# Semaphores allocated and cleared by the kernel itself, in two steps on GpSimd, instead of by the surrounding tile context

## The chip, the cores and the metric

One core of one Trainium2 chip. The metric is device microseconds of one execution. The profiled execution is one run of its own; the other times are of runs without a profile.

## The reference

What is computed is a low-rank update that is added to its input, for 16 x 512 = 8192 tokens of width 768, with rank 16:

```python
def reference(x, A, B, scale):
    lora = np.matmul(np.matmul(x, A), B)
    return (x + scale * lora).astype(np.float32)
```

x and the output are float32 and 25.2 MB each; A and B are 48 KB each.

## The kernel before, in words

The tokens are cut into five parts of 8, 8, 16, 16 and 16 tiles of 128 tokens (`PARTS`, L14). SyncE issues every transfer (`on_sync`, L126): seven loads of x, one of A, one of B, and six stores. The buffer `x_all` holds 48 of the 64 tiles, so the last part's two loads wait until the first two stores have landed (`s_out0`, `s_out1`, L154 to L157). Work goes in eight groups of eight tiles. For each group ScalarE and GpSimd narrow x to float16 (`narrowed`, L163, instruction at L171), VectorE transposes the group (L229), TensorE multiplies by A (`projected`, L260) and by B (`raised`, L281), ScalarE moves the small product between the two with the scale (L217), and VectorE adds the result to x in place (`summed`, L234). TensorE runs the first seven groups in a loop (L302). The order on each engine is written out by hand, and engines wait for one another on semaphores with names that begin with `s_`.

The end of the kernel matters here. `s_sum` counts the groups at whose end a store may go; its sixth count comes with the last sum. SyncE waits for it before each store (L133) and issues the last store (L137), which counts in `s_out` like the three before it. All of the body stands in a critical section of the tile context, opened at L124 and closed at L320. Ahead of the close GpSimd waits until `s_out` is 64, that is, until the last four stores have landed (L319). The wait is carried by GpSimd's jump out of the section, which the profile puts at L124. Behind the jump GpSimd and SyncE pass a no-operation to each other (L124). Then the tile context closes (L351): a barrier of all engines, a clear of a range of semaphores by GpSimd, and a second barrier. The semaphores come from `tc.alloc_semaphore` (L77 and L78), so they belong to the tile context, and its clear covers them: numbers 99 to 129 are the kernel's 31, and 130 to 135 are six of the context's own, for the start and the end of the section.

Of the kernel before, what the change touches and what calls it, by code (L numbers as in the profile page):

```python
# [24 lines left out]
def kernel(  # L25
# [8 lines left out]
    nc = tc.nc  # L34
# [19 lines left out]
    def ps(name, shape):  # L54
        return nc.alloc_psum_tensor(name, shape, fp32).ap()
# [18 lines left out]
    lora = [ps(f"lora_ps{i}", [P, 2, D]) for i in range(2)]  # L74
    y_ps = ps("ps_yt", [P, GROUP, Q])

    def sem(name):  # L77
        return tc.alloc_semaphore(name)  # L78


    parts = []
# [14 lines left out]
    def tiles(t, n):  # L96
# [3 lines left out]
        (0, 0, 2), (0, 2, 6), (1, 0, 8), (2, 0, 16), (3, 0, 16), (4, 0, 8), (4, 8, 8)  # L100
    ]
    s_load = [sem(f"s_load{k}") for k in range(len(LOADS))]

    def load_of(t):
        i, s = where[t]
        return next(k for k, ld in enumerate(LOADS) if ld[0] == i and ld[1] <= s < ld[1] + ld[2])

    s_a, s_b = sem("s_a"), sem("s_b")
    s_ready, s_brows, s_pick = sem("s_ready"), sem("s_brows"), sem("s_pick")
    s_w, s_bh, s_bp, s_bm = sem("s_w"), sem("s_bh"), sem("s_bp"), sem("s_bm")  # L110
    s_first, s_narrow, s_turned, s_taken = sem("s_first"), sem("s_narrow"), sem("s_turned"), sem("s_taken")
    s_y, s_spread, s_lora = sem("s_y"), sem("s_spread"), sem("s_lora")

    s_free = [sem(f"s_free{p}") for p in range(PAIRS)]
    s_sum = sem("s_sum")
    s_out0, s_out1, s_out = sem("s_out0"), sem("s_out1"), sem("s_out")

    MMS = 2 * NC
    STORES = [(0, 0, 8), (1, 0, 8), (2, 0, 16), (3, 0, 16), (4, 0, 8), (4, 8, 8)]
# [1 line left out]
    STORED = [where.index((i, s + n - 1)) // GROUP for i, s, n in STORES]  # L121
# [194 lines left out]
    on_vector(nc.vector)  # L316
    on_tensor(nc.tensor)

    nc.gpsimd.wait_ge(s_out, (len(STORES) - 2) * 16)  # L319
    section.close()  # L320


# [33 lines left out]
```

## Time and profile before

| | us |
|---|---|
| median of 3 runs | 124.40 |
| lowest and highest of them | 124.37, 124.55 |
| the profiled execution, its time | 124.31 |
| its span, first to last instruction | 122.5 |
| around its span | 1.8 |
| VectorE busy, share of the span | 81.8 (67%) |
| TensorE busy | 50.7 (41%) |
| ScalarE busy | 38.9 (32%) |
| GpSimd busy | 27.3 (22%) |

How to read it: the span runs from the first to the last instruction of the program on any engine, and what lies around it belongs to the runtime. Busy time counts an engine's work on data alone. Branches, semaphore instructions, clears and the issuing of transfers belong to an engine's queue (its sequencer). They are marked with a "q" behind the engine's name (POOLq is GpSimd's, SPq SyncE's, PEldq TensorE's) and are not counted as busy. In the answers for one line of the code, the columns are the shortest, the median and the longest duration in ns, and then the first and the last start in us. Where a start is given to three places, it is the record's own, in us from the span's start; the trace also holds an event for each write to a semaphore, with its number and time.

### The profile page before, as it was taken

Reading aid. Unit: us, or ns where it says so; the run is one execution under the profiler, and the core shown is the slowest. Engines: PE = TensorE matmul, PEld = TensorE weight load, DVE = VectorE, ACT = ScalarE, POOL = GpSimd, SP = SyncE. Lnnn points to the kernel's source line nnn. Section 1 sums busy time; section 2 is a strip of 40 time slices with the busy share of each in tenths; the row PEclk is TensorE's granted clock in tenths of the full one; section 3 lists DMA queues with packets and bytes.
Section 4 is the critical chain, followed back from the end, with each engine's and each line's share of the span. In section 5 each row is a group of like instructions: output and inputs, shape, how many; then the busy total and the mean of one; then the engine's idle time right before and its main releaser. Section 6 shows DMA issues by size and latency. Waiting matters only on the chain.

```text
span 122.5 us, 883 instructions
## 1 busy us (share of the span) xinstructions
PE 50.7 (41%) x322; PEld 29.9 (24%) x322; DVE 81.8 (67%) x42; ACT 38.9 (32%) x44; POOL 27.3 (22%) x25
## 2 busy tenths in 40 slices
PE   0000219477104974574574576477467432000000
PEld 0000017244002642442332334244244211000000
DVE  0000960799509999999999999999999599100000
ACT  4131946700094454444264083172300400000000
POOL 7500666200080440440260080071000000000000
PEclk9999999999965799999999999999999999855555
DMA  3999997996997997999999999999799799799990
GB/s 60 419 439 389 425 562 305 514 498 273 514 498 321 465 498 305 457 401 433 465 385 441 457 409 465 417 498 465 321 498 482 337 482 465 321 465 401 425 465 24
DMA packets 1928, 50.43 MB, mean 412 GB/s; under 512 B 236, under 2 KB 236, under 8 KB 392
## 3 DMA queue, kind: packets, MB, share of 16 engines
q1 hardware_dynamic: 1928, 50.43, 96.6%
HBM read 25.26 MB, written 25.17 MB: 412 GB/s over the span
## 4 chain that ended last, share of the span: by engine, by line
DVE 49%; DMA 24%; issue 4%; POOL 3%; PE 2%; SPq 2%; POOLq 0%; DVEq 0%
DVE x_sb L234 33%; DMA x_sb<-in_x_dram 24%; DVE xt L229 16%; POOL xn L171 2%; PE lora_ps L281 1%; PE ps_yt L260 1%; POOL a_rows L176 1%; SPq L142 1%; SPq L129 0%; SPq L146 0%; POOLq L351 0%; DVEq L247 0%; SPq L124 0%
## 5 line engine op out<-in xcount | busy, mean ns | idle before, releaser
L234 DVE TENSOR_TENSOR x_sb<-x_sb,lora_ps 128x1536 f32<-128x1536 f32 x32 | 53.7, 1735 | 1.4 <-PE lora_ps L281 1.4
L281 PE MATMUL lora_ps<-b_mm,y_bd 128*128 128x512 f16 (+1 forms) x128 | 26.1, 339 | 26.5 <-issue 18.8
L171 ACT CAST xn<-x_sb 128x3072 f16<-128x3072 f32 (+1 forms) x10 | 24.9, 2495 | 37.9 <-DMA x_sb<-in_x_dram 20.9
L229 DVE STREAM_TRANSPOSE xt<-xn 128x3072 f32<-128x3072 f32 (+1 forms) x9 | 27.1, 3007 | 9.3 <-POOL xn L171 9.0
L260 PE MATMUL ps_yt<-xt,w_bd 128*128 128x256 f16 x192 | 25.3, 282 | 11.5 <-DVE xt L229 11.5
L171 POOL CAST xn<-x_sb 128x3072 f16<-128x3072 f32 x7 | 19.2, 2748 | 46.4 <-PE ps_yt L260 32.8
L260 PEld LDWEIGHTS ps_yt<-xt,w_bd 128*128 128x128 f16 x192 | 18.7, 100 | 18.9 <-issue 14.6
L281 PEld LDWEIGHTS lora_ps<-b_mm,y_bd 128*128 128x128 f16 x128 | 11.0, 100 | 39.5 <-issue 21.6
L217 ACT ACTIVATE y_bd<-ps_yt 32x256 f16<-32x256 f32 x32 | 12.0, 374 | 19.0 <-PE ps_yt L260 18.7
L222 DVE STREAM_TRANSPOSE a_t<-a_rows 96x1024 f32<-96x1024 f32 x1 | 2.0, 1964 | 12.0 <-DMA a_rows<-in_A_dram 12.0
L293 PE MATMUL lora_ps<-b_half,pick 128*128 128x512 f16 (+1 forms) x2 | 0.8, 500 | 13.3 <-POOL b_half L188 13.3
L293 PEld LDWEIGHTS lora_ps<-b_half,pick 128*128 128x128 f16 x2 | 0.1, 106 | 13.3 <-issue 13.3
L188 POOL CAST b_half<-b_rows 128x768 f16<-128x768 f32 x1 | 0.8, 824 | 7.5 <-DMA b_rows<-in_B_dram 7.5
L198 POOL COPY w_bd<-w_one 32x384 f16<-32x384 f16 x4 | 2.0, 501 | 0.2
L171 ACT ACT_TABLE_LOAD x1 | 1.3, 1283 | 0.9 <-SPq L124 0.9
L192 POOL CAST w_one<-a_t 32x128 f16<-32x128 f32 x3 | 1.2, 397 | 1.0 <-DVE a_t L222 0.9
L179 POOL MEMSET w_bd<- 128x1536 f32 x1 | 1.4, 1382 | 0.0
L176 POOL MEMSET a_rows<- 96x1024 f32 x1 | 0.9, 948 | 0.5 <-SPq L124 0.5
L210 ACT CAST b_mm<-lora_ps 128x768 f16<-128x768 f32 x1 | 0.8, 798 | 0.0
L177 POOL MEMSET b_rows<- 128x768 f32 x1 | 0.7, 736 | 0.0
L180 POOL MEMSET y_bd<- 128x512 f32 x1 | 0.5, 524 | 0.0
L182 POOL TENSOR_SCALAR_AFFINE_SELECT pick<-pick 128x128 f16<-128x128 f16 x1 | 0.3, 309 | 0.0
(5 smaller groups left out, 0.6 us busy)
## 6 DMA issues: line engine op xcount, KB each, us to landing
x_sb<-in_x_dram SPq DMA_DIRECT2D x2, 6144.0 KB, 36.8
out_dram<-x_sb SPq DMA_DIRECT2D x4, 3072.0 KB, 17.2
out_dram<-x_sb SPq DMA_DIRECT2D x2, 6144.0 KB, 22.9
x_sb<-in_x_dram SPq DMA_DIRECT2D x3, 3072.0 KB, 14.7
x_sb<-in_x_dram SPq DMA_DIRECT2D x1, 2304.0 KB, 10.4
x_sb<-in_x_dram SPq DMA_DIRECT2D x1, 768.0 KB, 4.7
a_rows<-in_A_dram SPq DMA_DIRECT2D x1, 48.0 KB
b_rows<-in_B_dram SPq DMA_DIRECT2D x1, 48.0 KB, 9.4
```

What stands on the lines that cost most here:

```text
L142: e.dma_start(out=a_rows[0 : NC * APART : APART, :], in_=A.rearrange("(c e) r -> c (e r)", e=64)).then_inc(s_a, 16)
L171: ins = copy(out=xn[:, ds(first, n), :], in_=tiles(t, n))
L176: e.memset(a_rows[0 : NC * APART], 0.0).then_inc(s_ready, 1)
L179: e.memset(w_bd.rearrange("p c k m -> p (c k m)").bitcast(fp32), 0.0)
L192: e.tensor_copy(out=w_one[:, ds(b * EACH, EACH), :, :], in_=a_t[ds(b * Q, Q)].rearrange("i k r (c n) -> i c k r n", n=APART)[..., 0],).the ...
L198: e.tensor_copy(out=w_bd[ds(b * Q, Q), :, :, ds(b * Q, R)], in_=w_one).then_inc(s_w, 1)
L217: last = e.mul(out=y_bd[q, :, q], in_=y_ps[q, :, :], mul=sc)
L222: e.transpose(out=a_t[0 : NC * APART].rearrange("i k r c -> i (k r) c"), in_=a_rows[0 : NC * APART].rearrange("c (i k r) -> c (k r) i", k= ...
L229: return e.transpose(out=ts[0], in_=ts[1])
L234: ins = e.tensor_tensor(out=xs, in0=xs, in1=lora[p % 2], op=mybir.AluOpType.add)
L260: mm = e.matmul(y_ps, w_bd[:, c, k, :], xv[:, :, c, :, k], start=(m == 0), stop=(m == MMS - 1),)
L281: mms.append(e.matmul(t[:, k, ds(n0, w)], y_bd[:, 2 * p + k, :], b_mm[:, ds(n0, w)], start=True, stop=True,))
```

## The change

The semaphores are taken from the core's allocator (`nc.alloc_semaphore`) and not from the tile context, which therefore no longer clears them. `s_sum` is moved behind `s_out0` and `s_out1`, so that the 29 others have the numbers 99 to 127, and `s_sum` and `s_out` have 128 and 129. At the end GpSimd waits until `s_sum` is 6 (the last sum is made) and clears 99 to 127. Then it waits until `s_out` is 64 and clears 128 and 129. The section's close and the context's close follow as before; the context's clear is left with 130 to 135.

```diff
+    sems = []
+
     def sem(name):
-        return tc.alloc_semaphore(name)
+        sems.append(nc.alloc_semaphore(name))
+        return sems[-1]
...
-    s_sum = sem("s_sum")
-    s_out0, s_out1, s_out = sem("s_out0"), sem("s_out1"), sem("s_out")
+    s_out0, s_out1 = sem("s_out0"), sem("s_out1")
+
+    s_sum, s_out = sem("s_sum"), sem("s_out")
...
+    nums = [s.num for s in sems]
+    assert nums == list(range(nums[0], nums[0] + len(nums))) and sems[-2:] == [s_sum, s_out]
+
+    nc.gpsimd.wait_ge(s_sum, len(STORED))
+    nc.gpsimd.sem_clear(range(nums[0], s_sum.num))
     nc.gpsimd.wait_ge(s_out, (len(STORES) - 2) * 16)
+    nc.gpsimd.sem_clear(range(s_sum.num, s_out.num + 1))
     section.close()
```

In the program that is built, GpSimd's first clear carries the wait for `s_sum` and the second the wait for `s_out`. The jump out of the section, which carried the wait for `s_out` before, waits for nothing now. The other engines' instructions are the same in number and order.

## The prediction

> **What bounds the kernel now.** I read the row of the DMA engines first, then the chain of waits at its end, then the last microseconds instruction by instruction. The span's 40 slices (3.06 us each) show the transfers busy from the second slice to the last but one; the only queue is at 96.6% of the 16 engines' span:
>
> ```profile
> span 122.5 us, 883 instructions
> ...
> DMA  3999997996997997999999999999799799799990
> ...
> q1 hardware_dynamic: 1928, 50.43, 96.6%
> ```
>
> The chain, followed in time, ends with VectorE's last four sums:
>
> ```profile
> 97.76 6.75 DVE x_sb L234 x4
> ```
>
> That is 97.76 + 6.75 = 104.51 us, 18 us ahead of the end. All that comes behind it is the last stores (the last one issued at 104.5) and a tail. The stretches of the last three microseconds show where data stop:
>
> ```profile
> 119.80:120.20 0.40, 0.00 (x0) 0.00 (x0) 0.00 (x0) 0.00 (x0) 0.00 (x0) 0.50 0.30 123
> 120.20:120.60 0.40, 0.00 (x0) 0.00 (x0) 0.00 (x0) 0.00 (x0) 0.00 (x0) 0.50 0.00 0
> 120.60:121.00 0.40, 0.00 (x0) 0.00 (x0) 0.00 (x0) 0.00 (x0) 0.00 (x0) 0.50 0.00 0
> 121.00:122.50 1.50, 0.00 (x0) 0.00 (x0) 0.00 (x0) 0.00 (x0) 0.00 (x0) 0.50 0.00 0
> ```
>
> (The last two columns are the DMA share and GB/s.) From 121.0 on no engine works and nothing moves: 1.5 us of the span are queue instructions alone. By the semaphore events, the last of `s_out`'s 64 counts arrives at 121.288. SyncE has waited for GpSimd since 105.2, in the queue's own waits:
>
> ```profile
> SPq L124 <- POOLq L124: 16.3, 1, 16.3
> ```
>
> So from 121.288 to 122.492 the time is one serial row of small instructions on GpSimd's and SyncE's queues, and each ns taken out of it or put into it moves the end by one. These are the answers for L124 and for L351, cut to GpSimd:
>
> ```profile
> L124 POOLq COMPARE_BRANCH  x1: 33/33/33, 121.3 to 121.3; - x1
> L124 POOLq NOP  x1: 13/13/13, 121.5 to 121.5; - x1
> ```
>
> ```profile
> L351 POOLq EVENT_SEMAPHORE  x4: 17/17/17, 121.7 to 122.4; - x4
> L351 POOLq DRAIN  x3: 34/41/104, 121.6 to 122.2; - x3
> ...
> L351 POOLq EVENT_SEMAPHORE_RANGE_CLEAR  x1: 243/243/243, 122.0 to 122.0; - x1
> ```
>
> The reader is to see two things in that row: a branch that waits for the stores (start 121.312, the next instruction only at 121.474), and one clear of 243 ns (121.954 to 122.197).
>
> **The change, part by part.**
>
> *The allocator, the new numbers, the first wait and the first clear (29 semaphores).* Nothing. GpSimd's last work on data is over long before the last sum (none of it in any stretch from 104 us on). It now waits from then until 104.5, clears, and waits again. Queued behind the first wait are only the second clear and the tail, and those wait for `s_out` until 121.3 anyway: 16.8 us of cover, against 243 ns for a larger clear. No engine but GpSimd waits for it before the tail. Without that cover it would cost up to 243 ns. SyncE's last store waits for the same count of `s_sum`, which this clear leaves alone.
>
> *The last clear, 37 semaphores to 6.* The trace has the 37 writes one by one: number 99 at 121.974 (20 ns behind the clear's start), then four writes within 5 ns and a step of 21.7 ns to the next four, number 135 at 122.169 (28 ns ahead of its end). So 195 of the 243 ns go by the count, and 48 are fixed. Six semaphores are one step: 20 + 23 + 28 = 71 ns. Saved: 243 - 71 = **172 ns**. From both sides: a clear can hardly be shorter than the shortest semaphore instruction beside it, 17 ns (saved 226), or longer than the larger one (saved 0). I take 71, since it is read from the same instruction's own writes.
>
> *The branch.* It takes 162 ns from its start to the next instruction: 33 for itself and 129 until GpSimd's queue goes on. Its wait now sits on the second clear, and what is left is a jump to the code that stands next. The profile has no record for any jump of that kind: before, each engine has one at the head of the program and others at the end of the section, and GpSimd has two COMPARE_BRANCH records in all, both with a wait. Nor is there room for one: SyncE's last store ends at 104.865 and its next instruction, with such a jump between, starts at 104.902. So I take the 162 ns as gone. From the other side: if it stays, it costs 162 at most.
>
> *The second clear, 2 semaphores.* New on the serial row. It starts when the branch did, at 121.312. By the writes above, 20 + 2 + 28 = 50 ns; bounds 17 and 243. Behind it comes the gap to the no-operation. Gaps on GpSimd's queue are 30 to 34 ns around the clear, 44 and 69 behind the other closing DRAINs, 61 to 64 behind instructions that count a semaphore, and 136 at the widest (behind a barrier, up to a wait). I take 40, near the clear's own 34, because a clear counts none: together 90 ns, where the branch took 162. Saved: **72 ns**.
>
> *DRAIN of 104 ns ahead of the last clear.* The other two closing ones take 41 and 34. It carries the range that is to be reset, and no semaphore of the range is written while it runs, so I leave it alone: 0, at best 104 - 34 = 70 saved.
>
> **Sum:** -172 - 72 = -244 ns. From the profiled execution, 124.31 - 0.24 = 124.07; its time is 0.09 below the median of the runs shown, 124.40, which is what a new median is held against: 124.40 - 0.24 = **124.16 us**. That is 0.196%, so it stands on the line of 0.2% (0.25 us) which is about what a measurement of this kernel can tell from no change.
>
> Two rules of the skill would give other sums. The Trainium skill, "Runtime: NRT & Kernel Launch", section "The launch sequence", puts about 1.5 us on the reset of 51 semaphores per engine; as an estimate from that page 29 ns each, so that 31 fewer would save 0.9 us. The row here speaks against it: all 37 take 243 ns. The Trainium skill, "Advanced Engine Details and Errata", section "Control Flow Timing", gives about 108 ns for a compare-and-branch; by that the branch's part would be 108 - 90, and the sum -0.19 us. The row here has 162.
>
> **The rivals.**
>
> 1. *The jump stays, without its wait.* Then the second clear is put on top: 90 - 172 = -82 ns, 124.40 - 0.08 = 124.32. For it: the instruction is still in the program. Against it: no jump without a wait has a record outside TensorE's loop. Chance 0.10.
> 2. *The DRAIN shrinks with its range.* -244 - 70 = -314 ns at most, 124.09. For it: the two that carry no range are 63 and 70 ns shorter. Chance 0.09.
> 3. *A clear costs the same whatever its count, and the jump goes.* The last one saves nothing, the second costs 243 + 40 where the branch took 162: +121 ns, 124.52. Against it: 195 ns between the first write and the last. Chance 0.03.
> 4. *Slower: the same fixed cost, and the jump stays.* The place is the row behind the last count of `s_out`, where two clears then stand in place of one: +243 + 34 = +277 ns, 124.68. With a fixed part F of each clear and (243 - F)/37 for each semaphore, the second clear, its gap of 34 and the last clear equal 243 at F = 200 ns; from there on the change loses. The writes put F at 48. Chance 0.03, and 0.01 for an unseen loss of that size.
>
> That the tile context goes on clearing all 37 would leave -72 ns (124.33); the built program's last clear has six, so it has no chance of its own.
>
> **How the numbers follow.** The forecast has 0.74. Its time is on the line, and the runs before differ by 0.18 us, so I split it nearly in half: 0.41 faster by over 0.2%, 0.33 within. Rival 2 adds 0.09 to faster; rivals 1 and 3 add 0.13 to within: faster 0.50, within 0.46, slower 0.04. For the range, the low end is all bounds at their best: clears of 17 ns each and a gap of 30 (47 - 162 - 226 = -341) and the shorter DRAIN (-70), -411 ns, so 123.99, and 0.03 for the lowest run's distance from the median: 123.96. The high end is rival 1, 124.32, with half of the runs' spread, 0.09: 124.41. What lies above (rivals 3 and 4 and the upper bounds of the two clears) is left out: under 1 in 10.
>
> **What would show it.** At L351 GpSimd's clear should be about 71 ns, not 243; at the lines of the two new waits there should be clears of about 50 ns at the end and of about 48 + 29 x 5.3 = 200 near 104.6; GpSimd should have one COMPARE_BRANCH left, at 0.8 us; the no-operation should start about 90 + 24 ns behind the last count of `s_out`, where it was 186. The DRAIN stays at 104. From the last count to the span's end it should be 1204 - 244 = 960 ns. I would be wrong if the clear at L351 stays over 200 ns, if a branch is still recorded near 121, or if the last count itself comes at another time than 121.3 by more than the runs' spread: the transfers are the same, and nothing in the change reaches them.

## The result, and the profile after

| | before | after |
|---|---|---|
| median, us (22 runs each) | 124.43 | 124.24 |
| lowest and highest | 124.25, 124.64 | 123.97, 124.54 |
| profiled execution, its time | 124.31 | 124.27 |
| its last count of `s_out`, from the span's start | 121.288 | 121.546 |
| from there to the span's end (the tail), ns | 1204 | 910 |
| from the span's end to the last semaphore event, ns | 1941 | 1938 |

The ratio of after to before is 0.9984, with a 95% interval of 0.9977 to 0.9992: faster by about 0.2 us, less than the 0.2% that was taken as the line, and clear of no change. Ratios here and below are to the kernel before, over all runs of the two kernels, and differ a little from the ratio of the two medians. One execution of all those below, of the kernel with 64 more semaphores, took 127.38 us at a granted clock of 0.617, where the others of that kernel have 0.887 to 0.900, and is left out of its ratio.

The page of the kernel after has the same picture as before: one more instruction, the same transfers, the same busy row of the DMA engines.

```profile
span 122.5 us, 884 instructions
...
DMA  3999997996997996999999999999899799699990
...
q1 hardware_dynamic: 1928, 50.43, 96.7%
```

The span is as long as before, to the tenth. That is no contradiction: the stores landed 258 ns later in this execution, and the tail behind them is 294 ns shorter. The place to look is again the row of queue instructions, in the answers for L327 and L329 (the two new clears), L128 (the section, L124 before) and L361 (the context's close, L351 before), cut to GpSimd:

```profile
L327 POOLq EVENT_SEMAPHORE_RANGE_CLEAR  x1: 200/200/200, 105.0 to 105.0; - x1
```

```profile
L329 POOLq EVENT_SEMAPHORE_RANGE_CLEAR  x1: 45/45/45, 121.6 to 121.6; - x1
```

```profile
L128 POOLq NOP  x1: 13/13/13, 121.7 to 121.7; - x1
```

```profile
L361 POOLq EVENT_SEMAPHORE  x4: 17/17/17, 121.8 to 122.4; - x4
L361 POOLq DRAIN  x3: 34/41/64, 121.7 to 122.2; - x3
...
L361 POOLq COMPARE_BRANCH  x1: 33/33/33, 0.8 to 0.8; - x1
L361 POOLq EVENT_SEMAPHORE_RANGE_CLEAR  x1: 67/67/67, 122.1 to 122.1; - x1
```

The reader is to see four things. The large clear runs at 105.0, 16.5 us ahead of the stores' landing. The branch at 121 is gone: L128 has none on GpSimd's queue, and the one that is left is at the start. The last clear is 67 ns, not 243. And the longest DRAIN is 64 ns, not 104, which the forecast had left alone.

### The profile page after: what moved, and what is told of

Its sections match the earlier page's. It is cut to its first block, busy times and chain, and to the rows that moved or that the text cites. A ratio compares the mean times of both kernels' runs of the same rounds, so it can differ in the third digit from the quotient of the medians.

```text
span 122.5 us, 884 instructions
## 1 busy us (share of the span) xinstructions
PE 52.4 (43%) x322; PEld 30.8 (25%) x322; DVE 81.9 (67%) x42; ACT 39.0 (32%) x44; POOL 27.3 (22%) x25
## 4 chain that ended last, share of the span: by engine, by line
DVE 50%; PE 13%; issue 10%; DMA 8%; ACT 3%; SPq 0%
DVE x_sb L238 33%; DVE xt L233 18%; PE ps_yt L264 8%; DMA x_sb<-in_x_dram 8%; PE lora_ps L285 5%; ACT xn L175 3%; SPq L133 0%; SPq L361 0%; SPq L128 0%
## 5 line engine op out<-in xcount | busy, mean ns | idle before, releaser
L264 PE MATMUL ps_yt<-xt,w_bd 128*128 128x256 f16 x192 | 27.1, 296 | 11.6 <-DVE xt L233 11.6
L264 PEld LDWEIGHTS ps_yt<-xt,w_bd 128*128 128x128 f16 x192 | 19.6, 104 | 20.0 <-issue 14.7
```

What stands on the lines that cost most here:

```text
L264: mm = e.matmul(y_ps, w_bd[:, c, k, :], xv[:, :, c, :, k], start=(m == 0), stop=(m == MMS - 1),)
```

## The experiments

Two questions were left. Which part of the change gives what, and by what law? And why is the median 0.19 us lower when the profile shows 0.29 us less in the tail?

**The changed kernel again.** No edit.

> The changed kernel once more, unaltered, beside the others. What is open: the tail behind the last count of s_out is 910 ns in the profile after and 1204 before, 294 less, while the medians differ by about 0.19 us. Theory (the tail counts in full, the rest is scatter of the moment at which the last count comes): this profile has a tail of 905 to 915 again, the last count anywhere between 121.1 and 121.8, and the time is 0.2 to 0.35 us below the kernel before. Rival (the change makes the stores land later by 0.1): the last count is at 121.4 or later here and in every kernel with an early clear, and the time is 0.1 to 0.2 below.

Measured: 124.12 us against 124.41, ratio 0.9979 (0.9970 to 0.9989). The tail is 910 ns to the ns, the last count came at 121.373. The rival, stores that land later by some 0.1 us with an early clear in place, asks for 121.4 or later in every such kernel and misses that here by 27 ns. The median is 0.29 lower this time, where it asks for 0.1 to 0.2.

**One clear.** The early clear is taken out, and all 31 are cleared when the stores have landed:

```diff
-    nc.gpsimd.wait_ge(s_sum, len(STORED))
-    nc.gpsimd.sem_clear(range(nums[0], s_sum.num))
     nc.gpsimd.wait_ge(s_out, (len(STORES) - 2) * 16)
-    nc.gpsimd.sem_clear(range(s_sum.num, s_out.num + 1))
+    nc.gpsimd.sem_clear(range(nums[0], s_out.num + 1))
```

> No early clear: all 31 semaphores are cleared in one piece when the stores have landed. Theory (a clear costs about 45 to 48 ns and 21.7 for each further four semaphores): that clear takes about 200 ns where the one of two took 45, the tail is 910 + 155 = 1065 ns, and the time 0.14 us below the kernel before. Rival (a fixed cost for a clear, the gain being that of the branch alone): the clear takes 45 to 70 ns and the tail stays at 910 to 935.

Measured: 124.26 us, ratio 0.9993 (0.9984 to 1.0002). The clear's answer in the trace:

```profile
L327 POOLq EVENT_SEMAPHORE_RANGE_CLEAR  x1: 203/203/203, 121.3 to 121.3; - x1
```

203 ns for 31 where 45 stood for two, and a tail of 1074 ns. A clear's price goes by the count; the early clear is worth 164 ns of tail because it takes 29 semaphores off the serial row. The time does not stand clear of no change, so this reading rests on the tail.

**The branch alone.** To the kernel before, a semaphore instruction is added that carries the wait (nothing reads what it adds to `s_pick`):

```diff
     nc.gpsimd.wait_ge(s_out, (len(STORES) - 2) * 16)
+    nc.gpsimd.sem_inc(s_pick, 1)
```

> The kernel before with the wait for the stores taken off the jump: a semaphore instruction of GpSimd carries it, the tile context clears all as before. It tells the branch's part alone. Theory: no branch record near 121; 17 ns and a gap of about 61 in place of 162, so a tail of 1204 - 84 = 1120 ns, clear at 243, DRAIN at 104; time 0.08 us below. Rival (the jump stays and costs the same without its wait): a tail of 1204 + 78 = 1282 ns, time 0.08 above.

Measured: 124.31 us, ratio 0.9998 (0.9989 to 1.0008), which by itself tells nothing. The rows do: the answers for the new instruction and for the context's close.

```profile
L320 POOLq EVENT_SEMAPHORE  x1: 17/17/17, 121.3 to 121.3; - x1
```

```profile
L352 POOLq DRAIN  x3: 34/41/104, 121.4 to 122.1; - x3
...
L352 POOLq COMPARE_BRANCH  x1: 33/33/33, 0.8 to 0.8; - x1
L352 POOLq EVENT_SEMAPHORE_RANGE_CLEAR  x1: 243/243/243, 121.8 to 121.8; - x1
```

A jump that waits for nothing leaves no branch, as the forecast had it. From the new instruction's start to the next one it is 96 ns (17 and a gap of 79, not 61), where the branch took 162, and the tail is 1139 ns, 65 less. The clear and the DRAIN are those of before.

**More semaphores.** To the kernel before, 64 are added that nothing uses:

```diff
+    spare = [sem(f"spare{i}") for i in range(64)]
+
     MMS = 2 * NC
```

> The kernel before with 64 more semaphores that nothing uses, so that the tile context's clear has 101 in place of 37. It measures the clear's price by count, and whether the DRAIN ahead of it goes by its range. Theory: 25 steps of 21.7 and 48 = 590 ns for the clear, and the DRAIN, which was 104 for 37 and 64 for 6 (1.3 ns each), takes 104 + 83 = 187; tail 1204 + 347 + 83 = 1634, time 0.43 us above. Rival for the DRAIN (it is long when GpSimd clears for the first time, short when a clear came earlier): DRAIN 104, tail 1551, time 0.35 above. Rival for the clear (fixed cost): 243, no change.

Measured: 124.79 us, ratio 1.0038 (1.0026 to 1.0050). The context's close:

```profile
L353 POOLq DRAIN  x3: 34/41/198, 121.5 to 122.6; - x3
...
L353 POOLq EVENT_SEMAPHORE_RANGE_CLEAR  x1: 590/590/590, 122.0 to 122.0; - x1
```

590 ns was the forecast to the ns: 64 semaphores cost 347, 5.4 each. The DRAIN takes 198 (187 was expected), so it does go by its range, at 1.5 ns for each of the 64. The tail is 1644 ns, 440 more than before, and the time stands well clear of no change. No branch, early clear or wait differs here, so the price by count, of the clear and its DRAIN together, is shown by the time too.

**The early clear on SyncE.** SyncE, behind its last store, clears the 29. `s_sum` and `s_out` are the context's again, and the jump keeps its wait:

```diff
-    s_sum, s_out = sem("s_sum"), sem("s_out")
+    sems += [tc.alloc_semaphore("s_sum"), tc.alloc_semaphore("s_out")]
+    s_sum, s_out = sems[-2:]
...
-    nc.gpsimd.wait_ge(s_sum, len(STORED))
-    nc.gpsimd.sem_clear(range(nums[0], s_sum.num))
+    nc.sync.wait_ge(s_sum, len(STORED))
+    nc.sync.sem_clear(range(nums[0], s_sum.num))
     nc.gpsimd.wait_ge(s_out, (len(STORES) - 2) * 16)
-    nc.gpsimd.sem_clear(range(s_sum.num, s_out.num + 1))
```

> SyncE makes the early clear of 29 when the last sum is made, and s_sum and s_out are the tile context's again: its clear has 8 semaphores, the jump keeps its wait for the stores, and GpSimd makes no clear ahead of the context's. It takes the clear's part alone, and tells what shortens the DRAIN. Theory (DRAIN by range): branch 162 as before, clear of 8 in two steps 70 ns, DRAIN about 66; tail 1204 - 173 - 38 = 993 ns, time 0.21 us below the kernel before. Rival (the first clear of GpSimd has a long DRAIN ahead of it): DRAIN 104, tail 1031, time 0.17 below.

Measured: 124.16 us against 124.39, ratio 0.9987 (0.9976 to 0.9997). The early clear, the section's branch and the context's close:

```profile
L328 SPq EVENT_SEMAPHORE_RANGE_CLEAR  x1: 77/77/77, 105.6 to 105.6; - x1
```

```profile
L129 POOLq COMPARE_BRANCH  x1: 33/33/33, 121.5 to 121.5; - x1
```

```profile
L361 POOLq DRAIN  x3: 34/41/66, 121.8 to 122.2; - x3
...
L361 POOLq EVENT_SEMAPHORE_RANGE_CLEAR  x1: 74/74/74, 122.1 to 122.1; - x1
```

The DRAIN is 66 ns although GpSimd had cleared nothing before it, so the rival (the first clear has a long one ahead of it) falls. The branch is there, with its 161 ns to the next instruction, and the tail is 991 ns. This and the branch alone together (-213 and -65) come near the whole change (-294), whose instruction at the wait is a little cheaper, 89 ns for 96, and whose last clear has two semaphores fewer, 67 ns for 74.

**The wait last.** If the row behind the last count is paid in full, most of it can go. In the changed kernel the wait for the stores and the clear of two are moved behind the context's close:

```diff
-    nc.gpsimd.wait_ge(s_out, (len(STORES) - 2) * 16)
-    nc.gpsimd.sem_clear(range(s_sum.num, s_out.num + 1))
     section.close()
+    return s_sum, s_out, (len(STORES) - 2) * 16
...
     with _tile.TileContext(nc) as tc:
-        tile_lora_fused_kernel(tc, *args)
+        s_sum, s_out, landed = tile_lora_fused_kernel(tc, *args)
+    nc.gpsimd.wait_ge(s_out, landed)
+    nc.gpsimd.sem_clear(range(s_sum.num, s_out.num + 1))
```

> The changed kernel with the wait for the stores and the clear of two moved behind the tile context's close: both barriers and the context's clear run at about 105 us under the stores, and only the wait and the clear of two are left behind the last count. Theory (the serial row behind the last count is paid in full, whatever it holds): a tail of 24 + 45 = 70 ns in place of 910, time about 1.1 us below the kernel before and 0.84 below the changed one. Rival (what lies behind the last instruction waits for something else, such as the transfers' own end): the tail goes but the time falls by 0.5 us or less.

Measured: 123.45 us (123.28 to 123.96, 5 runs) against 124.39, ratio 0.9920 (0.9907 to 0.9934): faster than both kernels, and about 1.0 us below the one before, where 1.1 was expected. The profiled execution is the slowest of the five, 123.96. The context's close and the last clear:

```profile
L360 POOLq EVENT_SEMAPHORE  x4: 17/17/17, 106.7 to 107.2; - x4
...
L360 POOLq EVENT_SEMAPHORE_RANGE_CLEAR  x1: 67/67/67, 107.0 to 107.0; - x1
```

```profile
L363 POOLq EVENT_SEMAPHORE_RANGE_CLEAR  x1: 45/45/45, 122.0 to 122.0; - x1
```

Both barriers and the context's clear are over by 107.3, under the stores, and the tail is 69 ns. The rival, an end that waits for something else, falls: from the span's end to the last semaphore event it is 1992 ns, 51 more than before, and no more is given back there.

**All together.** The tail's part in the ratio is worked out as 1 + (tail - 1.204) / 124.4, tails in us:

| kernel | tail, ns | ratio by the tail | ratio measured, 95% interval | last count, us |
|---|---|---|---|---|
| before | 1204 | 1 | | 121.288 |
| after | 910 | 0.9976 | 0.9984 (0.9977 to 0.9992) | 121.546 |
| after, again | 910 | 0.9976 | 0.9979 (0.9970 to 0.9989) | 121.373 |
| one clear | 1074 | 0.9990 | 0.9993 (0.9984 to 1.0002) | 121.268 |
| branch alone | 1139 | 0.9995 | 0.9998 (0.9989 to 1.0008) | 121.235 |
| 64 more | 1644 | 1.0035 | 1.0038 (1.0026 to 1.0050) | 121.213 |
| early clear on SyncE | 991 | 0.9983 | 0.9987 (0.9976 to 0.9997) | 121.506 |
| wait last | 69 | 0.9909 | 0.9920 (0.9907 to 0.9934) | 122.024 |

Six of the seven intervals hold the tail's ratio; the first misses it by 0.0001. So the tail counts in full, as near as these runs can tell.

The last count moves by 0.8 us from execution to execution, though the transfers are the same in all of them. Each kernel has only one profile. Those with an early clear have the later counts here (121.373 to 122.024, against 121.213 to 121.288), but much of that lies in which execution was profiled: in the four kernels without an early clear it ran 0.10 to 0.13 us below its kernel's median, and in those with one it was 0.03 below to 0.51 above. The ratios use all runs and are the better sign. Each is above the tail's ratio: by 0.0003 in the three other kernels without an early clear, by 0.0003 and 0.0004 in "after, again" and with the early clear on SyncE, by 0.0008 in the first runs of the kernel after, and by 0.0011 with the wait last (0.0004 of it are the 51 ns at the end). The same kernel thus has 0.0008 and 0.0003, so the scatter between two sets of runs is about as large as the 0.1 us in question, and two of the four rows with an early clear show nothing of it. Whether it moves the last count a little is not settled. The record of the last store gives no cause: its issue takes 333 ns beside GpSimd's clear and 332 before, and SyncE's next instruction starts 37 ns behind it in both.

## Why the prediction was right

- **What bounds the end.** Right. The work on data ends with the stores, what lies behind their last count is serial, and a ns in it is a ns of the time. The runs with 64 more semaphores (slower) and with the wait last (faster), both by the tail's amount within their intervals, show that from both sides. The reading names GpSimd's and SyncE's queues alone; the barriers also take in the other engines, and the last instruction of the span is TensorE's, 51 ns from 122.441 on.
- **The first wait and the first clear: nothing.** Right. 200 ns at 105.0 (about 202 by the working), all of it under the stores.
- **The last clear: -172 ns.** Measured 243 to 67, so -176. The law read from one clear's 37 writes, steps of 21.7 ns for four, held to within 5 ns from 2 semaphores (50 by the law, 45 measured) to 101 (590 and 590).
- **The branch and the second clear: -72 ns.** Measured 162 to 89, so -73. The jump that waits for nothing has no record in any kernel here, so rival 1 falls.
- **The DRAIN: 0.** Here a term was mis-sized. It goes by the range that it carries, 64 ns for 6 semaphores, 66 for 8, 104 for 37 and 198 for 101, and gave 40 ns. Rival 2 had the mechanism, with 0.09, and at most 70. What misled the step is that none of the semaphores is written while the DRAIN runs; that the one DRAIN with a range was also the one long DRAIN was the better sign.
- **The sum: -244 ns** in the tail; measured -294, of which 289 are these three terms and 5 a shorter gap behind the last clear. The time forecast, 124.16 us, lies 0.08 below the first median and 0.04 above the second. That it comes so near the first is in part luck: the tail fell by 50 ns more than forecast, and the time by 0.1 us less than the tail. On which side of 0.2% the change falls was left even, and it stays so: the ratios are 0.9984 and 0.9979.
- **A sign of being wrong that did appear.** The last count came at 121.546, 0.26 us from 121.288, which is more than the 0.18 by which the three runs differed. That yardstick was too small: the 22 runs before differ by 0.39 us, and the unaltered kernel after had 121.373 the second time. That nothing in the change reaches the transfers is not shown to the last 0.1 us.
- **Rivals 3 and 4** (a fixed cost for each clear) fall with the 203 and 590 ns. One figure in rival 4 does not follow from its terms: 2F + 8 (243 - F)/37 + 34 = 243 gives F = 88 ns for the point of balance, not 200. The margin to the 48 read from the writes was thus smaller than it looked, and the measured clears still lie below it: the one of two took 45 ns in all.
- **The two rules.** The 29 ns for a semaphore that follow as an estimate from the Trainium skill, "Runtime: NRT & Kernel Launch", section "The launch sequence", where it is the runtime's own reset that is priced, are not what a clear over a range costs here: 5.4 ns on GpSimd. The Trainium skill, "Advanced Engine Details and Errata", section "Control Flow Timing", has about 108 ns for a compare-and-branch; here it is 161 or 162 from the start of the waiting branch at the section's end to the next instruction, in three kernels.

## What to carry to other kernels

Look behind the last transfer: what stands there is serial, no engine's busy time shows it, and here it was 1.2 us of 124.4, one per cent. What did not need the stores' landing here (barriers, clears, hand-overs between engines) could run while they were under way, with only the wait and a clear of two behind them; that was worth more (about 1 us) than making each of those instructions cheaper (0.3 us in the tail). Where an effect is at the edge of what the times can tell, the instruction's own record tells it to the ns, and one kernel that makes the suspected cost larger (64 more semaphores) lifts it out of the scatter.

## What the runs showed of the hardware

- The same clear of 29 semaphores takes 200 ns on GpSimd's queue and 77 on SyncE's. The semaphore events show where the time goes: SyncE writes one about each 1.7 ns without a break (47 ns from the first to the last of 29), GpSimd four within 5 ns and then nothing until about 21.7 ns have passed since the first of them (151 ns for the 29).
- When the last store is issued says little of when it has landed: issues at 104.451 to 105.822 in the eight profiles, last counts at 121.213 to 122.024, and the issue at 105.276 has the earliest of them.
